# One wide matmul for two products: the feature-major matrix products of a two-block network in float32 pairs

## The chip, the core and the metric

One core of one Trainium2 chip. The metric is device time in microseconds (us) for one execution of the program. TensorE (PE, with its weight loads as PEld) multiplies, VectorE (DVE) and ScalarE (ACT) read its results out of PSUM, GpSimd (POOL) works on SBUF, and SyncE (SP) issues the loads of weights.

## What is computed

256 tokens of 1024 features go through two blocks of two layers each. Cut to what matters:

```python
# first block, per layer
proj = rms_norm(x, norm1_g[l]) @ w_in[l]
x = x + concat([retention(...), stick_breaking(...)]) @ w_out[l]
h = rms_norm(x, norm2_g[l])
x = x + (silu(h @ w_gate[l]) * (h @ w_up[l])) @ w_down[l]
# second block, per layer
proj = rms_norm_2(x, g_mix[l]) @ w_in[l]        # latents, q/k/v of two attentions, gate logits
merged = gates[0] * (y_a @ w_pa[l]) + gates[1] * (y_b @ w_pb[l]) + gates[2] * (y_c @ w_pc[l])
x = x + merged @ w_o[l]
x = x + (silu(h @ w1[l]) * (h @ w3[l])) @ w2[l]  # h = rms_norm_2(x, g_ffn[l])
```

D_FF is 2816 in both blocks, so a feed-forward layer has 22 tiles of 128 hidden features and 8 of output features.

## The kernel before

All operands of the large products are float32 numbers split into two float32r parts, hi and lo (class `Pair`). A product is three matmuls, `mm3` (L253): hi x hi, hi x lo and lo x hi, in lines L255, L256 and L257. The weights come from memory in chunks of 128 x 1024 (`fetch`, L222, on SP's queue, four raw buffers); `split` makes hi on ACT (L237) and lo on DVE (L238), 512 columns at a time, four chunks ahead of their use.

There are two forms of product. In the token-major form (`tm`, L266) the activations are the stationary operand and 512 columns of weights move past them. In the feature-major form (`fm1`, L302, and `fm2`, L281) a weight tile of 128 x 128 is stationary and the 256 tokens of the activations move past it, once for hi and once for lo:

```python
mm(out, l.hi, r.hi, start=start, stop=False, skip_group_check=True)
mm(out, l.hi, r.lo, start=False, stop=False, skip_group_check=True)
mm(out, l.lo, r.hi, start=False, stop=stop, skip_group_check=True)
```

So each of the three lines loads its weight tile anew, the high one twice. `fm2` fills one PSUM bank with two output tiles of 256 columns. PSUM has four banks under the tag mm, two under sc and one each under pt and ov (`bank`, L262).

Feature-major products are: gate and up in `ffn` (L500 to L502, 8 k-tiles), down (L520, 22 k-tiles; the last layer's last two tiles one by one, L524 to L527), sq and sk of the first block's mixer (L578), and in the second block's mixer the gates (L856), q and k of the third attention (L920, L922), the branches (L865, 2 or 4 k-tiles), and w_o (L935). Two latent products go to sc banks (L732). The first block's w_out (L686 to L696) and the second block's latent up-projections (L892 to L913) call `mm3` themselves.

What reads a bank: in `ffn` DVE multiplies G by the row R of 1 / rms (L509), ACT takes silu, DVE multiplies by U (L512), and ACT and DVE split the result into hT's hi and lo (L514, L515). `add` (L447) multiplies by R if given (L454), adds to x (L456), and makes the next norm's xT (L384 on ACT, L385 on DVE) and squares; its instructions and branch c's last ones have a higher priority in the order of instructions. In `branch` (L863) DVE multiplies a bank by the gate (L868, L871); branch a's result is added to mg by POOL (L873), branch c's by DVE (L876), which then makes the pair mT.

The order of each engine's instructions is made by the framework's scheduler from the program's order, the priorities and the buffers that are free; each engine then runs its own instructions in that order.

Of the kernel before, what the change touches and what calls it, by code (L numbers as in the profile page):

```python
# [29 lines left out]
# Position p of the residual holds token TOK[p]: the tokens of one residue mod 4 lie together.  # L30
# [101 lines left out]
def tiles(a):  # L132
    """[256, ...] -> [128, 2, ...]"""
# [43 lines left out]
# ---------------------------------------------------------------- the program  # L177


class Pair:  # L180
    """A float32 tensor as the exact sum of two float32r tensors."""
# [7 lines left out]
    def rearrange(self, *a, **k):  # L189
        return Pair(self.hi.rearrange(*a, **k), self.lo.rearrange(*a, **k))  # L190


class Net:
# [16 lines left out]
    # ---- weights  # L210
# [31 lines left out]
    def chunk(self, inner, ahead=4):  # L242
        """The next chunk of the weights as [128, k-tiles, inner]."""
# [7 lines left out]
    # ---- matrix products  # L251
# [10 lines left out]
    def bank(self, tag="mm"):  # L262
        n = {"mm": 4, "sc": 2, "pt": 1, "ov": 1}[tag]
# [17 lines left out]
    def fm2(self, xT, tag="mm", nk=NKT):  # L281
        """Feature-major product with the next chunks: a bank [128, 2, 256] for two 128-column tiles."""
        out = self.half(tag)
        g = min(CW // 128, nk)
        if CW // (128 * g) >= 2:
            c = self.columns(g)
            for j in range(2):
                for k in range(nk):
                    self.mm3(out[:, j, :], c[:, j, k, :], xT[:, k, :], j + k == 0, k == nk - 1)
        else:  # L290
            for j in range(2):
# [10 lines left out]
    def fm1(self, out, xT, start, nk=NKT):  # L302
        g = CW // 128
        for k0 in range(0, nk, g):
            c = self.chunk(128)
            for k in range(min(g, nk - k0)):
                self.mm3(out, c[:, k, :], xT[:, k0 + k, :], start and k0 + k == 0, k0 + k == nk - 1)

    def evac_pair(self, ps, out, scale=None):
        """A PSUM tensor as an exact pair."""  # L310
# [11 lines left out]
    # ---- small things  # L322

    def gains(self, name, l=0, n=NKT):
        """The columns [128, n] of a gain of layer l."""
# [3 lines left out]
    def rsqrt(self, out, ssq, n):  # L329
        """out = (ssq / n + eps) ** -0.5"""  # L330
# [13 lines left out]
    def transposes(self, src, tag):  # L344
        """src [128 t, 4 * 128] -> a bank [128, 4, 128 t]."""
# [5 lines left out]
    # ---- the residual, its norms, and what is added to it  # L351
# [3 lines left out]
    def norm_start(self, g, natural=False, inner=None, last=False):  # L355
        """A norm of the residual x, k-tile by k-tile: n["T"] becomes x * g, transposed as x is, as a pair.
        What is made of it is still to be scaled by 1 / rms of the token."""
        n = {"g": g, "natural": natural, "inner": inner, "last": last}
        if last:
            n["y"] = self.act.tile([128, NKT, S], F32, tag="xTh", name="y")  # L360
        else:
            n["T"] = self.pair_tile(self.act, [128, NKT, S], "xT")
# [3 lines left out]
    def norm_part(self, n, m):  # L366
        """k-tiles m and m + 1 of x are ready."""
# [38 lines left out]
    def norm_sums(self, n):  # L406
        """The sums over the features, a column for each tile of tokens."""
# [9 lines left out]
    def norm_cols(self, n):  # L417
        """1 / rms as columns [128, 2]; if there is an inner norm, x is to become rms_norm(x, inner) first."""
# [15 lines left out]
    def norm_end(self, n):  # L434
        """1 / rms as columns and as a row on all partitions."""
# [11 lines left out]
    def add(self, b, m, n, R=None):  # L447
        """x += the bank b (scaled by R if given) for k-tiles m and m + 1; the next norm n goes on with them."""
# [606 lines left out]
```

## Time and profile before

| | |
|---|---|
| runs of the program | 1616.18, 1614.48, 1615.78 us; median 1615.78 |
| span of the profiled execution | 1613.9 us |
| PE busy | 1595.7 us, 12188 matmuls |
| PEld busy | 1530.2 us |
| DVE busy | 1049.8 us, 1852 instructions |
| ACT busy | 813.1 us, 1558 instructions |
| read from memory | 266.78 MB, 166 GB/s over the span |

A busy time is the union of an engine's instructions. Matmuls are pipelined: the record of one goes on while the next has begun, so the pace is the distance between starts. In the rows a DVE or ACT instruction is named by what it writes and reads (t<-mm,R), and an idle time by what ended it.

### The profile page before, as it was taken

The page shows a single profiled execution, that of the slowest core. Times are in us where ns is not written, and L with a number is a line of the kernel's source. Part 1 is how long each engine was busy: PE and PEld are TensorE (multiplying, and loading weights), DVE is VectorE, ACT ScalarE, POOL GpSimd, SP SyncE. Part 2 cuts the span into 40 slices and gives each one's busy share as a digit, 9 for nine tenths or more (in the row PEclk, how much of TensorE's full clock was granted, in tenths as well). Part 3 has the DMA queues.
Part 4 walks back from the last instruction along what each step waited for, and adds up shares of the span by engine and source line. Part 5 has one row for each costly group of instructions (what it writes and reads, how often), then busy time and mean ns, then how long its engine had stood idle before and what let it go on. Part 6 is the DMA issues. An engine that isn't in the chain of part 4 may idle for free.

```text
span 1613.9 us, 30319 instructions
## 1 busy us (share of the span) xinstructions
PE 1595.7 (99%) x12188; PEld 1530.2 (95%) x12188; DVE 1049.8 (65%) x1852; ACT 813.1 (50%) x1558; POOL 103.4 (6%) x117
## 2 busy tenths in 40 slices
PE   8999999999999999999999999999999999999997
PEld 7889999997999999899999999999899999999997
DVE  7767565667765656776567766656676567765653
ACT  6545444455554545455444554445455444554442
POOL 2001000100110003100001000001000001100001
PEclk9999999999999999999999999999999999999998
DMA  7445555654455556532534555556532544555551
GB/s 265 171 153 179 183 183 168 197 173 133 163 175 183 181 177 209 181 127 90 183 126 156 183 180 184 180 171 209 177 122 92 183 134 151 181 183 183 177 180 63
DMA packets 78653, 269.81 MB, mean 167 GB/s; under 512 B 8624, under 2 KB 12848, under 8 KB 78384
## 3 DMA queue, kind: packets, MB, share of 16 engines
q1 hardware_dynamic: 78224, 267.34, 50.7%
q8 instruction: 96, 1.57, 0.4%
q10 hardware_dynamic: 288, 0.52, 0.1%
q14 instruction: 45, 0.37, 0.1%
HBM read 266.78 MB, written 1.05 MB: 166 GB/s over the span
## 4 chain that ended last, share of the span: by engine, by line
PE 71%; DVE 0%; POOL 0%; ACT 0%; issue 0%; DVEq 0%; ACTq 0%; POOLq 0%
PE mm L255 21%; PE mm L257 20%; PE mm L256 20%; PE ov L260 3%; PE sc L260 3%; PE pt L348 2%; PE pt L260 1%; PE sc L255 0%; PE sc L256 0%; PE sc L257 0%; PE pt L801 0%; POOL acc L404 0%; DVE y L1018 0%; ACT p L784 0%; POOL rr L335 0%
## 5 line engine op out<-in xcount | busy, mean ns | idle before, releaser
L237 ACT CAST hi<-raw 128x512 fp32r<-128x512 f32 x1004 | 567.7, 611 | 633.7 <-issue 415.8
L238 DVE TENSOR_TENSOR lo<-raw,hi 128x512 fp32r<-128x512 f32 x1004 | 667.6, 701 | 311.6 <-ACT hi L237 308.2
L255 PE MATMUL mm<-xTh,hi 128*128 128x256 f32 x2048 | 582.5, 285 | 0.0
L256 PE MATMUL mm<-xTl,hi 128*128 128x256 f32 x2048 | 581.0, 284 | 0.9 <-DVE xTl L385 0.9
L257 PE MATMUL mm<-xTh,lo 128*128 128x256 f32 x2048 | 581.5, 284 | 0.0
L256 PEld LDWEIGHTS mm<-xTl,hi 128*128 128x128 f32 x2048 | 392.9, 192 | 1.6 <-DVE xTl L385 1.3
L255 PEld LDWEIGHTS mm<-xTh,hi 128*128 128x128 f32 x2048 | 392.5, 192 | 0.5
L257 PEld LDWEIGHTS mm<-xTh,lo 128*128 128x128 f32 x2048 | 392.5, 192 | 0.3
L255 PE MATMUL mm<-hTh,hi 128*128 128x256 f32 x704 | 199.2, 283 | 0.0
L256 PE MATMUL mm<-hTl,hi 128*128 128x256 f32 x704 | 199.2, 283 | 0.0
L257 PE MATMUL mm<-hTh,lo 128*128 128x256 f32 x704 | 199.2, 283 | 0.0
L256 PE MATMUL mm<-lo,xTh 128*128 128x512 f32 (+1 forms) x352 | 136.2, 387 | 1.8 <-DVE lo L238 1.8
L255 PE MATMUL mm<-hi,xTh 128*128 128x512 f32 (+1 forms) x352 | 136.2, 387 | 1.4 <-ACT hi L237 1.4
L257 PE MATMUL mm<-hi,xTl 128*128 128x512 f32 (+1 forms) x352 | 136.4, 388 | 0.0
L255 PEld LDWEIGHTS mm<-hTh,hi 128*128 128x128 f32 x704 | 135.2, 192 | 0.0
L256 PEld LDWEIGHTS mm<-hTl,hi 128*128 128x128 f32 x704 | 135.2, 192 | 0.0
L257 PEld LDWEIGHTS mm<-hTh,lo 128*128 128x128 f32 x704 | 135.2, 192 | 0.0
L256 PEld LDWEIGHTS mm<-lo,xTh 128*128 128x128 f32 x352 | 66.8, 190 | 14.9 <-DVE lo L238 3.3
L255 PEld LDWEIGHTS mm<-hi,xTh 128*128 128x128 f32 x352 | 66.6, 189 | 13.1 <-ACT hi L237 1.9
L257 PEld LDWEIGHTS mm<-hi,xTl 128*128 128x128 f32 x352 | 66.7, 190 | 11.4
L404 POOL TENSOR_TENSOR acc<-acc,sq 128x256 f32<-128x256 f32 x58 | 52.9, 914 | 180.1 <-ACT sq L395 177.9
L512 DVE TENSOR_TENSOR h<-mm,t 128x512 f32<-128x512 f32 x44 | 30.4, 692 | 45.4 <-PE mm L257 42.3
(216 smaller groups left out, 1883.8 us busy)
## 6 DMA issues: line engine op xcount, KB each, us to landing
raw<-w SPq DMA_DIRECT2D x470, 512.0 KB, 3.4
raw<-w SPq DMA_DIRECT2D x32, 384.0 KB, 3.2
bias<-bias SPq DMA_DIRECT2D x16, 256.0 KB, 3.2
c<-c SPq DMA_DIRECT2D x1, 1088.0 KB, 6.4
x<-x SPq DMA_DIRECT2D x4, 256.0 KB, 5.9
c<-c SPq DMA_DIRECT2D x1, 768.0 KB, 7.3
out<-y SPq DMA_DIRECT2D x2, 256.0 KB, 2.3
out<-y ACTq DMA_DIRECT2D x2, 256.0 KB, 2.9
```

The source lines that it names most:

```text
L237: nc.scalar.copy(out=hi[:, c], in_=raw[:, c])
L238: nc.vector.tensor_tensor(out=lo[:, c], in0=raw[:, c], in1=hi[:, c].bitcast(F32), op=ALU.subtract)
L255: mm(out, l.hi, r.hi, start=start, stop=False, skip_group_check=True)
L256: mm(out, l.hi, r.lo, start=False, stop=False, skip_group_check=True)
L257: mm(out, l.lo, r.hi, start=False, stop=stop, skip_group_check=True)
L260: self.nc.tensor.matmul(out, l, r, start=start, stop=stop, skip_group_check=True)
L348: self.nc.tensor.transpose(b[:, k, :], src[:, 128 * k:128 * (k + 1)], self.k["ident"])
L404: nc.gpsimd.tensor_tensor(out=acc, in0=acc, in1=t, op=ALU.add)
L512: nc.vector.tensor_tensor(out=h, in0=U, in1=t, op=ALU.mult)
```

## The change

The hi and lo parts of an activation tensor come to lie side by side in one tile (`Twin`), [128, k, 2, 256]. A feature-major product is then two matmuls (`mmw`): the high weight tile with 512 columns, hi and lo of the activations, into the two halves of a bank, and the low weight tile with the 256 columns of hi into the first half. An output tile takes a bank of its own, a pair of them two banks (`quad`). On the way out ACT copies the second halves to SBUF (`second`) and DVE adds the first halves to them (`whole`); what was done with the bank before is done with the sum. The four mm banks become two buffers of two banks. The weights of gate and up are fetched two chunks of one, then two of the other. The products into sc banks, w_out's and the latents' stay as they are.

```diff
 def lay_ffn(wg, wu, wd):
     out = []
-    for a, b in zip(lay_fm(wg), lay_fm(wu)):
-        out += [a, b]
+    g, u = lay_fm(wg), lay_fm(wu)
+    for j in range(0, len(g), 2):
+        out += g[j:j + 2] + u[j:j + 2]
...
+class Twin(Pair):
+    def __init__(self, t):
+        super().__init__(t[:, :, 0, :], t[:, :, 1, :])
+        self.both = t
...
+    def banks(self):
+        return self.ps.tile([128, 2, 512], F32, tag="mm", bufs=2, name="mm")
...
     def tm(self, xT, nk, n=512, then=None):
-        out = [self.bank() for _ in range(2)]
+        b = self.banks()
+        out = [b[:, i, :] for i in range(2)]
...
+    def mmw(self, out, w, x, k, start, stop):
+        mm = self.nc.tensor.matmul
+        flat = lambda t: t.rearrange("p a t -> p (a t)")
+        mm(flat(out), w.hi, flat(x.both[:, k, :, :]), start=start, stop=False, skip_group_check=True)
+        mm(out[:, 0, :], w.lo, x.hi[:, k, :], start=False, stop=stop, skip_group_check=True)
+
+    def wide1(self, out, xT, nk=NKT):
+        g = CW // 128
+        for k0 in range(0, nk, g):
+            c = self.chunk(128)
+            for k in range(min(g, nk - k0)):
+                self.mmw(out, c[:, k, :], xT, k0 + k, k0 + k == 0, k0 + k == nk - 1)
+
+    def quad(self):
+        return self.banks().rearrange("p e (a t) -> p e a t", a=2)
+
+    def wide2(self, xT, nk=NKT):
+        out = self.quad()
         g = min(CW // 128, nk)
         if CW // (128 * g) >= 2:
             c = self.columns(g)
             for j in range(2):
                 for k in range(nk):
-                    self.mm3(out[:, j, :], c[:, j, k, :], xT[:, k, :], j + k == 0, k == nk - 1)
+                    self.mmw(out[:, j], c[:, j, k, :], xT, k, k == 0, k == nk - 1)
         else:
             for j in range(2):
-                self.fm1(out[:, j, :], xT, j == 0, nk)
+                self.wide1(out[:, j], xT, nk)
         return out
...
+    def second(self, b):
+        t = self.act.tile([128, 2, S], F32, tag="part", bufs=2, name="part")
+        t = t[:, :b.shape[1], :]
+        self.nc.scalar.copy(out=t, in_=b[:, :, 1, :])
+        return t
+
+    def whole(self, out, b):
+        self.nc.vector.tensor_tensor(out=out, in0=b[:, :, 0, :], in1=self.second(b), op=ALU.add)
+        return out
...
             if R is not None:
                 t = self.act.tile([128, 2, S], F32, tag="sq", bufs=2, name="t")
-                nc.vector.tensor_tensor(out=t, in0=b, in1=R.unsqueeze(1).to_broadcast([128, 2, S]), op=ALU.mult)
-                b = t
-            nc.vector.tensor_tensor(out=x, in0=b, in1=x, op=ALU.add)
+                self.whole(t, b)
+                nc.vector.tensor_tensor(out=t, in0=t, in1=R.unsqueeze(1).to_broadcast([128, 2, S]), op=ALU.mult)
+                nc.vector.tensor_tensor(out=x, in0=t, in1=x, op=ALU.add)
+            elif len(b.shape) == 4:
+                t = self.second(b)
+                nc.vector.tensor_tensor(out=x, in0=b[:, :, 0, :], in1=x, op=ALU.add)
+                nc.vector.tensor_tensor(out=x, in0=t, in1=x, op=ALU.add)
+            else:
+                nc.vector.tensor_tensor(out=x, in0=b, in1=x, op=ALU.add)
             self.norm_part(n, m)
...
-                G, U = self.half(), self.half()
-                for e in range(2):
-                    self.fm1(G[:, e, :], xT, e == 0)
-                    self.fm1(U[:, e, :], xT, e == 0)
-                    if j + e == 0:
-                        self.norm_cols(n)
+                G = self.wide2(xT)
+                U = self.quad()
+                self.wide1(U[:, 0], xT)
+                if j == 0:
+                    self.norm_cols(n)
+                self.wide1(U[:, 1], xT)
...
-                nc.vector.tensor_tensor(out=t, in0=G, in1=Rb, op=ALU.mult)
+                self.whole(t, G)
+                nc.vector.tensor_tensor(out=t, in0=t, in1=Rb, op=ALU.mult)
                 nc.scalar.activation(out=t, in_=t, func=AF.Silu)
                 h = pool.tile([128, 2, S], F32, tag="h2", bufs=2, name="h2")
-                nc.vector.tensor_tensor(out=h, in0=U, in1=t, op=ALU.mult)
+                self.whole(h, U)
+                nc.vector.tensor_tensor(out=h, in0=h, in1=t, op=ALU.mult)
...
             def branch(name, nk, th, to=None):
                 for m in range(0, NKT, 2):
-                    b = self.fm2(yT[name], nk=nk)
+                    b = self.wide2(yT[name], nk=nk)
                     c = mg[:, m:m + 2, :]
                     if name == "b":
-                        nc.vector.scalar_tensor_tensor(out=c, in0=th[m // 2], scalar=1.0, in1=b, op0=ALU.add, op1=ALU.mult)
+                        self.whole(c, b)
+                        nc.vector.scalar_tensor_tensor(out=c, in0=th[m // 2], scalar=1.0, in1=c, op0=ALU.add, op1=ALU.mult)
                         continue
                     t = pool.tile([128, 2, S], F32, tag="bias", bufs=3, name="mt")
-                    nc.vector.scalar_tensor_tensor(out=t, in0=th[m // 2], scalar=1.0, in1=b, op0=ALU.add, op1=ALU.mult)
+                    self.whole(t, b)
+                    nc.vector.scalar_tensor_tensor(out=t, in0=th[m // 2], scalar=1.0, in1=t, op0=ALU.add, op1=ALU.mult)
...
-                    b = self.bank().rearrange("p (a t) -> p a t", a=2)
+                    b = self.banks()[:, 0, :].rearrange("p (a t) -> p a t", a=2)
...
```

`add_last`, sq and sk, the gates, and q and k of the third attention are changed like `ffn`'s G: `whole` first, then the operation of before on the sum. The pairs xT, hT, yT and mT become twins; mT takes the place that qa and ka had, which now lie in one tile.

## Rows read from the trace of the kernel before

**Rows 1.** The page, parts 1 and 4: busy times, and the chain that ended last

```profile
span 1613.9 us, 30319 instructions
...
PE 1595.7 (99%) x12188; PEld 1530.2 (95%) x12188; DVE 1049.8 (65%) x1852; ACT 813.1 (50%) x1558; POOL 103.4 (6%) x117
...
PE 71%; DVE 0%; POOL 0%; ACT 0%; issue 0%; DVEq 0%; ACTq 0%; POOLq 0%
```

**Rows 2.** Waits of the weight loads: us in total, times, longest; first and last of 19

```profile
PEld ov L260 <- DVE pT L790: 4.4, 14, 0.3
...
PEld sc L260 <- ACT ka L891: 0.3, 2, 0.2
```

**Rows 3.** Timeline of a down product: start us, us, engine, line, operation

```profile
262.17 0.28 PE L255 MATMUL mm<-hTh,hi 128*128 128x256 f32 x1
262.17 0.19 PEld L256 LDWEIGHTS mm<-hTl,hi 128*128 128x128 f32 x1
...
262.53 0.28 PE L255 MATMUL mm<-hTh,hi 128*128 128x256 f32 x1
```

**Rows 4.** Timeline of token-major products, and of the step to feature-major ones

```profile
400.18 0.39 PE L255 MATMUL mm<-hi,xTh 128*128 128x512 f32 x1
...
400.86 0.39 PE L255 MATMUL mm<-hi,xTh 128*128 128x512 f32 x1
...
807.08 0.39 PE L257 MATMUL mm<-hi,xTl 128*128 128x512 f32 x1
...
807.31 0.28 PE L255 MATMUL mm<-yTh,hi 128*128 128x256 f32 x1
...
807.42 0.28 PE L256 MATMUL mm<-yTl,hi 128*128 128x256 f32 x1
```

**Rows 5.** Busy us of PE, PEld, DVE, ACT, POOL by stretch; PEclk, DMA share, GB/s

```profile
20.00:50.00 30.00, 30.00 (x231) 29.00 (x230) 22.99 (x41) 16.69 (x31) 0.58 (x1) 1.00 0.82 288
134.00:260.00 126.00, 125.58 (x1046) 125.36 (x1046) 75.88 (x123) 60.98 (x110) 2.43 (x3) 1.00 0.55 178
...
864.00:868.00 4.00, 4.00 (x35) 4.00 (x35) 4.00 (x6) 2.06 (x4) 1.68 (x1) 1.00 0.45 146
```

**Rows 6.** Groups by line and form: count, busy us, mean ns

```profile
L255 PE MATMUL mm<-xTh,hi 128*128 128x256 f32 x2048 | 582.5, 285 | 0.0
...
L255 PE MATMUL mm<-hTh,hi 128*128 128x256 f32 x704 | 199.2, 283 | 0.0
```

**Rows 7.** The same groups, for DVE and ACT reading a full bank

```profile
L509 DVE TENSOR_TENSOR t<-mm,R 128x512 f32<-128x512 f32 x44 | 30.4, 691 | 40.5 <-PE mm L257 40.5
...
L646 ACT COPY rk<-pt 128x512 f32<-128x512 f32 x4 | 2.4, 588 | 4.0 <-PE pt L348 4.0
```

**Rows 8.** Timeline of DVE and PE from branch c into w_o, second block, layer 0

```profile
899.49 0.69 DVE L871 SCALAR_TENSOR_TENSOR mt<-th,mm 128x512 f32<-128x512 f32 x1 [1.06 <-PE mm L257]
...
907.86 0.28 PE L255 MATMUL mm<-mT,hi 128*128 128x256 f32 x1
...
908.79 0.68 DVE L871 SCALAR_TENSOR_TENSOR mt<-th,mm 128x512 f32<-128x512 f32 x1
...
909.99 0.69 DVE L876 TENSOR_TENSOR mt<-mg,mt 128x512 f32<-128x512 f32 x1
...
911.37 0.69 DVE L317 SCALAR_TENSOR_TENSOR mT<-mt,mT 128x512 fp32r<-128x512 f32 x1
```

**Rows 9.** Groups: POOL's additions of branch a; timeline: two weight splits on DVE beside them

```profile
L873 POOL TENSOR_TENSOR mg<-mg,mt 128x512 f32<-128x512 f32 x8 | 13.3, 1658 | 349.7 <-DVE mt L871 349.7
...
862.07 2.39 DVE L238 TENSOR_TENSOR lo<-raw,hi 128x512 fp32r<-128x512 f32 x2
```

**Rows 10.** Timeline of PE at the step from w_out to gate and up

```profile
134.81 0.39 PE L256 MATMUL mm<-xTl,hi 128*128 128x256 f32 x1 [0.42 <-DVE xTl L385]
```

**Rows 11.** The chain that ended last, near its end: start us, us, what

```profile
1602.89 0.44 DVE t L464
...
1607.56 0.38 ACT R L1012
```

More of the change, by code (lines that the diff above doesn't have):

```diff
@@ L279, with fm2 @@
     STATS = 1
-    def fm2(self, xT, tag="mm", nk=NKT):
+    def fm2(self, xT, tag, nk=NKT):
         out = self.half(tag)
[L284 to L288, printed above, removed]
-                    self.mm3(out[:, j, :], c[:, j, k, :], xT[:, k, :], j + k == 0, k == nk - 1)
-        else:
-            for j in range(2):
-                self.fm1(out[:, j, :], xT, j == 0, nk)
+        g = CW // 128
+        for j in range(2):
+            for k0 in range(0, nk, g):
+                c = self.chunk(128)
+                for k in range(min(g, nk - k0)):
+                    self.mm3(out[:, j, :], c[:, k, :], xT[:, k0 + k, :], j + k0 + k == 0, k0 + k == nk - 1)
         return out
@@ L306, in fm1 @@
             for k in range(min(g, nk - k0)):
-                self.mm3(out, c[:, k, :], xT[:, k0 + k, :], start and k0 + k == 0, k0 + k == nk - 1)
+                self.mmw(out, c[:, k, :], xT, k0 + k, k0 + k == 0, k0 + k == nk - 1)
[3 more added lines that the diff above has]
+        out = self.quad()
+        g = min(CW // 128, nk)
+        if CW // (128 * g) >= 2:
+            c = self.columns(g)
+            for j in range(2):
+                for k in range(nk):
+                    self.mmw(out[:, j], c[:, j, k, :], xT, k, k == 0, k == nk - 1)
+        else:
+            for j in range(2):
+                self.wide1(out[:, j], xT, nk)
[7 more added lines that the diff above has]
+        self.nc.vector.tensor_tensor(out=out, in0=b[:, :, 0, :], in1=self.second(b), op=ALU.add)
+        return out
     def evac_pair(self, ps, out, scale=None):
@@ L469, in add_last, with half @@
             nc.scalar.mul(out=n["y"][:, j, :], in_=x, mul=n["g"][:, j:j + 1])
[L471 removed]
+    def half(self, tag):
         return self.bank(tag).rearrange("p (a t) -> p a t", a=2)
@@ L519, in ffn @@
                     break
-                self.add(self.fm2(hT, nk=NFT), m, n2, R)
+                self.add(self.wide2(hT, nk=NFT), m, n2, R)
             else:
                 return n2
-            for j in (NKT - 2, NKT - 1):
-                b = self.bank()[:, :S]
-                self.fm1(b, hT, True, NFT)
-                self.add_last(b, j, n2, R)
+            b = self.quad()
+            for j in (0, 1):
+                self.wide1(b[:, j], hT, NFT)
+                self.add_last(b[:, j:j + 1], NKT - 2 + j, n2, R)
             return n2
@@ L577, in mixer1 @@
                 for j in range(2):
-                    b = self.fm2(xT)
-                    nc.vector.scalar_tensor_tensor(out=t[:, 2 * j:2 * j + 2, :], in0=b, scalar=sc, in1=Rb, op0=ALU.mult, op1=ALU.mult)
+                    u = t[:, 2 * j:2 * j + 2, :]
+                    self.whole(u, self.wide2(xT))
+                    nc.vector.scalar_tensor_tensor(out=u, in0=u, scalar=sc, in1=Rb, op0=ALU.mult, op1=ALU.mult)
                 sT.append(t)
@@ L685, in mixer1 @@
                 retention_gate(hp, os[hp])
-            banks = [self.half() for _ in range(NKT // 2)]
+            banks = [t[:, i, :].rearrange("p (a t) -> p a t", a=2) for t in [self.banks() for _ in range(NKT // 4)] for i in range(2)]
             for part in (4, 0):
@@ L855, in gates @@
                     t = pool.tile([128, 2, S], F32, tag="th", bufs=4, name="th")
-                    nc.vector.tensor_tensor(out=t, in0=self.fm2(xT), in1=Rb, op=ALU.mult)
+                    self.whole(t, self.wide2(xT))
+                    nc.vector.tensor_tensor(out=t, in0=t, in1=Rb, op=ALU.mult)
                     nc.scalar.activation(out=t, in_=t, func=AF.Tanh, scale=0.5)
@@ L904, in mixer2 @@
             for j in range(2):
-                b = self.half()
+                b = self.banks()[:, 0, :].rearrange("p (a t) -> p a t", a=2)
                 for e in range(2):
@@ L909, in mixer2 @@
                     nc.scalar.copy(out=kav[p, 2 * j:2 * j + 2, e, :], in_=b[p])
+            b = self.banks()
             for i in range(2):
-                b = self.bank()
-                self.mm3(b, latT[:, 2, 128 * i:128 * (i + 1)], w[:, 1, :], True, True)
-                nc.scalar.copy(out=va[:, i, :], in_=b)
+                self.mm3(b[:, i, :], latT[:, 2, 128 * i:128 * (i + 1)], w[:, 1, :], True, True)
+                nc.scalar.copy(out=va[:, i, :], in_=b[:, i, :])
             wide("a", qa, ka, va, lambda h: h, 96 ** -0.5, None)
@@ L919, in mixer2 @@
             for j in range(2):
-                nc.vector.scalar_tensor_tensor(out=qn[:, 2 * j:2 * j + 2, :], in0=self.fm2(xT), scalar=0.125, in1=Rb, op0=ALU.mult, op1=ALU.mult)
+                u = qn[:, 2 * j:2 * j + 2, :]
+                self.whole(u, self.wide2(xT))
+                nc.vector.scalar_tensor_tensor(out=u, in0=u, scalar=0.125, in1=Rb, op0=ALU.mult, op1=ALU.mult)
             for j in range(2):
-                b = self.fm2(xT)
+                b = self.act.tile([128, 2, S], F32, tag="sq", bufs=2, name="kn")
+                self.whole(b, self.wide2(xT))
                 u = kdv[:, 2 * j:2 * j + 2, :, :]
@@ L930, in mixer2 @@
             branch("a", 4, gates())
-            mT = Pair(*(pool.tile([128, NKT, S], F32R, tag=t, name="mT") for t in ("qa", "ka")))
+            mT = self.twin_tile(pool, NKT, "qk")
             branch("c", 4, gates(), mT)
@@ L934, in mixer2 @@
             for m in range(0, NKT, 2):
-                self.add(self.fm2(mT), m, n2)
+                self.add(self.wide2(mT), m, n2)
             return n2
```

33 lines of the change are left out of this document (18 added, 15 removed).

## The prediction

> **What bounds the kernel now.** I read the page first. TensorE (PE) is busy for 99% of a span of 1613.9 us, and the chain that ended last is 71% PE, with "0%" at every other engine [rows 1]. Matmuls overlap in the records, so a busy share alone does not prove a full engine; the waits of its weight loads do. That list has 19 rows, adds up to some 30 us, and its longest row is 4.4 us in total, its shortest 0.3 us [rows 2]. So PE hardly waits for anybody, and only what shortens its own stream can shorten the run. A microsecond on VectorE (DVE) or ScalarE (ACT) counts only where it makes PE wait.
>
> What paces that stream is read from starts, not from durations. One 256-column product, three matmuls, starts at 262.17 and the next at 262.53 [rows 3]: 120 ns a matmul, though each lasts 280 ns. In a token-major stretch 512-column matmuls start at 400.18 and, three later, at 400.86 [rows 4]: 226.7 ns each. Twice the columns cost 106.7 ns more, which is 256 columns at 2.4 GHz (the granted clock is 1.00 in the gate and up stage [rows 5]). So each weight load with its matmul costs 106.7 ns per 256 columns **plus a fixed 13.3 ns**, at either width, and that fixed part is what the change can save. Where a 512-column matmul is followed by 256-column ones, the starts are 807.08, 807.31, 807.42 [rows 4]: the wide one takes 0.23, the narrow one behind it 0.11 to 0.12. Mixing widths costs nothing extra there.
>
> **The change, part by part.**
>
> *The products.* Per k-tile and 128 output columns three loads and three matmuls of 256 (360 ns) become two loads with matmuls of 512 and 256: 226.7 + 120 = 346.7 ns. The same columns pass, one fixed part is gone: 13.3 ns. The products concerned are those on xT into mm banks (2048) and on hT (704) [rows 6], and by their loops those on yT (2 layers x 8 tiles x (2 + 4 + 4) k-tiles = 160) and mT (2 x 8 x 8 = 128): 3040 in all. The 64 on xT into sc banks, those on mixT and the latents keep three matmuls. 3040 x 13.3 ns = **40.5 us** less, and since PE has no slack to hide it in, all of it is on the path.
>
> The Trainium skill, "TensorE: Matmul & The Clock Gate", section "Back-to-back issue gap", has the isolated gap as N / 2.4 + 2.5 ns, so 109 ns for 256 columns and 216 for 512. The trace disagrees with 120 and 226.7 [rows 3, 4]; by that page of the Trainium skill the saving would be an estimate of 3040 x 2.5 ns = 7.6 us. I keep the trace's number.
>
> *The way out.* Each pair of output tiles now has its two halves in two banks, so it needs one more ACT copy (second) and one more DVE operation (whole, or the second addition in add). Pairs: 88 for gate and up, 15 and two single tiles for down, 8 for sq and sk, and 64 in the second block's mixers: 175 and two singles. An ACT copy of 512 from PSUM lasts 588 ns, a DVE operation of 512 lasts 691 ns [rows 7], but queued DVE operations of that size start 0.60 us apart (three in a row from 908.79 to 909.99, the middle one a weight split [rows 8]). So ACT gains 175 x 0.59 = 103 us and DVE 175 x 0.60 = 105 us: ACT from 813 to 916 us, DVE from 1050 to 1155 us [rows 1], 73% of the new span. Neither becomes the bound as a whole. What matters is each stage.
>
> *Gate and up.* The stretch 134 to 260 has DVE at 75.9 of 126 us [rows 5]. 22 pairs add 13.2 us, so some 89 of 122. A pair's banks are taken again only after the other product has run, 16 x 347 ns = 5.5 us; evacuation needs 0.59 + 0.60. I cost this at nothing; the cover is those 5.5 us, and without it each pair would cost up to 1.2 us. *Down, sq and sk* are the same with 15.3 and 5.5 us per pair: nothing. Token-major products had two of four banks each, now one of two double banks; a product lasts 48 x 226.7 ns = 10.9 us against an evacuation of two operations: nothing. The new order of the weight chunks moves no work: the same chunk arrives every 2.77 us in place of 2.88, 189 GB/s, where the trace has 178 in the gate and up stage and 288 in an early one [rows 5].
>
> *The second block's branches* are the tight place, because there a pair has few k-tiles. Per layer:
> - Branch b (2 k-tiles): PE 4 x 347 = 1.39 us a pair; DVE one weight split, the sum and the product, 3 x 0.60 = 1.80. Over four pairs DVE falls 1.6 us behind. Bounds 0 to 1.6, taken 0.7, as a pair can be one buffer late.
> - Branch a (4 k-tiles): PE 2.77 us a pair. POOL adds into mg at the same time, 1.66 us each [rows 9], and two weight splits then take 2.39 us in place of 1.2; DVE is busy all of 864 to 868 [rows 5, 9]. With sum and product DVE needs 2.39 + 1.20 = 3.6 us a pair: behind by 0.8, over four pairs 3.3. Bounds 0 to 3.3, taken 1.5.
> - Branch c: DVE goes without a gap from 899.49 to 912.06 [rows 8], 12.6 us for 11.5 us of PE. The product after it (w_o) starts at 907.86 and uses k-tiles 0 to 5 of two output tiles first, 12 x 360 ns = 4.3 us, which is just until the last part of mT is written, 911.37 + 0.69 = 912.06. After, the cover is 4.2 us, and DVE has four sums more, 2.4 us, with an ACT copy of 0.6 ahead of the last. Bounds 0 to 3.4 (0 if the weight splits queued in between give way), taken 1.6, the middle, since half of that queue is splits for later chunks.
> - From w_o into the feed-forward: the last addition gets an ACT copy and a DVE addition longer, 0.59 + 0.60 = 1.2 us with a wait. At the same kind of boundary PE already sat 0.42 us waiting for xTl [rows 10]. Bounds 0 to 1.3, taken 0.6.
> - The q projection uses one bank of each double bank, so two in flight, not four. Bounds 0 to 2.7 (four evacuations of 0.69), taken 0.5, near the low end because attention fills PE there.
>
> That is 4.9 us a layer (0 to 12.3), **9.8 us** for two (0 to 24.6); below nothing is excluded, since each of the five only adds instructions or takes buffers away. What waits behind is PE's in-order queue, and next the transposes of attention, whose copies stand in the same DVE queue.
>
> *The tail.* add_last gets a copy of 256 by ACT (0.38, as R's) and a sum by DVE (0.44) on the last chain [rows 11], with issue some **0.9 us**, all exposed.
>
> Sum on the profiled execution: 1613.9 - 40.5 + 9.8 + 0.9 = 1584.1 us. The median of the runs, 1615.78, is 1.9 us above that span, so **1586.0 us**, 1.8% less.
>
> **Rivals.**
> 1. *Evacuation in line (slower).* With two double banks in place of four banks, PE could wait at each pair for copy and sum. Price 1.2 us x 175 = 210 us, less 40.5: 1785 us. It decides from 40.5 / 175 = 0.23 us of exposure per pair. For it: DVE is without a gap in branch c [rows 8]. Against: in gate, up and down, 103 of the pairs, 5.5 us or more pass before a buffer is wanted. Chance 0.04.
> 2. *The saving is not there.* If 120 ns at 256 columns were set by the weight load, and the load behind a narrow matmul held up the next wide one, the change would not do what it says: 1615.8 + 10.7 = 1626.5. For it: a load lasts 0.19 us, more than the 0.12 between starts [rows 3]. Against: the fixed part is the same at 512 columns, where a load has ample time [rows 4]. Chance 0.03. The Trainium skill's 2.5 ns would end close by: 1626.5 less the estimate of 7.6 is 1619.
> 3. *The mixers' queues cost more than the bounds*, 25 to 37 us beside the tail, because instruction order there is chosen anew and attention waits for DVE: 1576 + 25 to 37 = 1601 to 1613. For: DVE is full in the branches [rows 8, 9]. Against: the stretches that are short of DVE today are two of some 12 us a layer. Chance 0.07.
>
> The forecast's own case, 0 to 25 us exposed, has 0.85, and 0.01 remains for a better one.
>
> **The numbers.** The low end takes no exposure but the tail: 1615.8 - 40.5 + 0.9 = 1576, and 1 for run to run: 1575. The high end takes all bounds: 1601. Outside lie rivals 1 to 3, 0.14. A difference of 0.2% (3.2 us) is about the least that a measurement of this kernel can tell from none. Faster by more: 0.85 + 0.07 + 0.01 = 0.93; slower: most of rivals 1 and 2, 0.05; within: 0.02.
>
> **What would show it.** Wide and narrow starts in gate and up alternate at 227 and 120 ns, and a pair of tiles (16 products) takes 5.55 us in place of 5.76; 11 rounds of gate and up take 122 us where they took 126.7. PE's matmul count falls by 3040. ACT is near 916 and DVE near 1155 us. The branches show PE waiting for part, mT or mm banks by 2 to 4 us a layer. I am wrong if the wide start-to-start is over 235 ns, if the feed-forward stages show PE waiting for DVE, or if the mixers lose over 25 us.

## The result and the profile after

The changed kernel takes **1598.26 us** (median of four runs, 1596.3 to 1601.81), against 1615.98 for the kernel before beside it: ratio 0.9896, 95% interval 0.988 to 0.9912. That is 17.7 us less, inside the range, but the predicted gain was 29.8. The profiled execution has a span of 1594.5 us (its own time 1596.3, the shortest of the four), 19.4 less than [rows 1]. One execution of experiment 1 below, which took 8426 us, is left out of its median.

The page of the changed kernel, parts 1, 4 and 5:

```profile
span 1594.5 us, 24578 instructions
...
PE 1564.0 (98%) x9148; PEld 1365.2 (86%) x9148; DVE 1148.7 (72%) x2029; ACT 897.1 (56%) x1735; POOL 110.5 (7%) x117
...
PE 91%; DVE 5%; POOL 1%; ACT 1%; issue 1%; DMA 0%; DVEq 0%; POOLq 0%; ACTq 0%
...
L317 PE MATMUL mm<-xT,hi 128*128 128x512 f32 x2048 | 719.8, 394 | 2.1 <-DVE mt L355 1.2
...
L350 ACT COPY part<-mm 128x512 f32<-128x512 f32 x177 | 102.4, 578 | 9.6 <-PE mm L318 9.6
```

PE's matmuls fall from 12188 to 9148, 3040 as counted. DVE gains 99 us and ACT 84 us. DVE now has 5% of the chain that ended last, where it had none [rows 1].

Timeline of gate and up in the changed kernel (start us, us, engine, line, operation):

```profile
179.66 0.39 PE L317 MATMUL mm<-xT,hi 128*128 128x512 f32 x1
179.89 0.28 PE L318 MATMUL mm<-xT,lo 128*128 128x256 f32 x1
180.01 0.39 PE L317 MATMUL mm<-xT,hi 128*128 128x512 f32 x1
...
181.05 0.39 PE L317 MATMUL mm<-xT,hi 128*128 128x512 f32 x1
```

Four products take 181.05 - 179.66 = 1.39 us, 347 ns each, the wide start to the narrow one 0.23: as predicted, where it was 360 [rows 3]. So the 40.5 us were saved, and 40.5 - 19.4 = **21.1 us came back elsewhere**. Where, is read from the first and last matmul of each stage in the two timelines (us; due: the stage's products times 13.3 ns):

| stage | before | due | after | came back |
|---|---|---|---|---|
| first block, mixer with gate and up, layers 0 and 1 | 260.01, 250.60 | 5.5 less each | 254.54, 245.94 | 0.0, 0.9 |
| down, each of the first three layers | 63.24 | 2.35 less | 60.90 | 0.0 |
| second block, mixer, layer 0 | 293.97 | 5.3 less | 296.20 | 7.5 |
| the same, layer 1 | 289.41 | 5.3 less | 292.78 | 8.7 |
| second block, gate and up (each) | 127.75 | 4.7 less | 123.65, 123.65 | 0.6 each |
| down, last layer | 63.24 | 2.35 less | 62.24 | 1.35 |
| from the last down matmul to the end | 11.41 | none | 12.82 | 1.4 |

Three quarters, 16.2 us, lie in the two mixers of the second block (the row of a mixer begins at the last matmul of the stage before). The waits of the weight loads in the changed kernel (us in total, times, longest) name the places:

```profile
PEld pt L269 <- POOL acc L456: 6.8, 4, 2.2
PEld mm L317 <- DVE qk L366: 6.2, 4, 1.6
PEld mm L317 <- DVE mt L355: 4.5, 6, 1.0
...
PEld mm L317 <- DVE mg L355: 2.8, 6, 0.5
```

The last three did not exist before, where the longest row was 4.4 us [rows 2], and they add up to 13.5 us. All of it is in these two mixers: mg is branch b, mt branch a and the banks that branch c's sums still read, and qk (the tile that mT now lies in) w_o waiting for mT. By stretch, one layer has 1.4 us behind the pairs of branch b, 1.7 behind those of branch a, and 3.1 + 0.6 in w_o. The products of branch c lose nothing (32 products in 11.14 us, from 881.25 to 892.39); what VectorE is late with there is paid in w_o, as PE's timeline of layer 0 shows (in brackets the idle time and what ended it):

```profile
894.40 0.50 PE L317 MATMUL mm<-qk,hi 128*128 128x512 f32 x1 [1.16 <-DVE qk L366]
895.61 0.50 PE L317 MATMUL mm<-qk,hi 128*128 128x512 f32 x1 [0.24 <-DVE mt L355]
900.00 0.50 PE L317 MATMUL mm<-qk,hi 128*128 128x512 f32 x1 [1.32 <-DVE qk L366]
```

The rest of the mixers' loss, 0.6 and 1.5 us, and the first block's 0.9 come ahead of the wide products, at **the step from down into the next mixer**. From the last matmul of down to the first feature-major product of the next mixer the kernel before takes 12.77, 15.76 and 12.07 us, the changed one 13.92, 16.35 and 13.59, which is 3.3 us more. There the last pair's copy and sum stand on the way to x, and behind it come the squares and POOL's sum of them (acc), for which PE waits. It is the first row of the list above; in the kernel before it reads:

```profile
PEld pt L260 <- POOL acc L404: 4.1, 5, 1.7
```

The three steps add up to 40.6 us before and 43.9 after, and to 39.0 and 40.6 in experiments 3 and 4 below, which have no copy and no sum there.

### The profile page after: what moved, and what is told of

Read it like the earlier page. It is cut to its first block, busy times and chain, and to the rows that moved or that the text cites. A ratio compares the mean times of both kernels' runs of the same rounds, so it can differ in the third digit from the quotient of the medians.

```text
span 1594.5 us, 24578 instructions
## 1 busy us (share of the span) xinstructions
PE 1564.0 (98%) x9148; PEld 1365.2 (86%) x9148; DVE 1148.7 (72%) x2029; ACT 897.1 (56%) x1735; POOL 110.5 (7%) x117
## 4 chain that ended last, share of the span: by engine, by line
PE 91%; DVE 5%; POOL 1%; ACT 1%; issue 1%; DMA 0%; DVEq 0%; POOLq 0%; ACTq 0%
PE mm L317 41%; PE mm L318 21%; PE mm L264 6%; PE mm L266 6%; PE mm L265 6%; PE sc L269 4%; PE ov L269 3%; PE pt L400 2%; DVE lo L247 1%; PE pt L269 1%; DVE mt L355 1%; POOL mg L939 1%; DVE mt L937 1%; POOL acc L456 0%; PE sc L264 0%
## 5 line engine op out<-in xcount | busy, mean ns | idle before, releaser
L317 PE MATMUL mm<-xT,hi 128*128 128x512 f32 x2048 | 719.8, 394 | 2.1 <-DVE mt L355 1.2
L318 PE MATMUL mm<-xT,lo 128*128 128x256 f32 x2048 | 577.1, 282 | 0.0
L317 PEld LDWEIGHTS mm<-xT,hi 128*128 128x128 f32 x2048 | 383.3, 187 | 86.8 <-DVE mt L355 1.9
L318 PEld LDWEIGHTS mm<-xT,lo 128*128 128x128 f32 x2048 | 387.1, 189 | 0.8
L317 PE MATMUL mm<-hT,hi 128*128 128x512 f32 x704 | 244.5, 391 | 0.6 <-DVE t L355 0.6
L318 PE MATMUL mm<-hT,lo 128*128 128x256 f32 x704 | 197.1, 280 | 0.0
L264 PE MATMUL mm<-hi,xT 128*128 128x512 f32 (+1 forms) x352 | 137.4, 390 | 1.0 <-ACT hi L246 1.0
L265 PE MATMUL mm<-lo,xT 128*128 128x512 f32 (+1 forms) x352 | 136.8, 389 | 1.5 <-DVE lo L247 1.5
L266 PE MATMUL mm<-hi,xT 128*128 128x512 f32 (+1 forms) x352 | 136.5, 388 | 0.0
L318 PEld LDWEIGHTS mm<-hT,lo 128*128 128x128 f32 x704 | 133.1, 189 | 0.0
L264 PEld LDWEIGHTS mm<-hi,xT 128*128 128x128 f32 x352 | 67.1, 191 | 13.4 <-ACT hi L246 1.5
L266 PEld LDWEIGHTS mm<-hi,xT 128*128 128x128 f32 x352 | 67.0, 190 | 12.0
```

The source lines that it names most:

```text
L317: mm(flat(out), w.hi, flat(x.both[:, k, :, :]), start=start, stop=False, skip_group_check=True)
L318: mm(out[:, 0, :], w.lo, x.hi[:, k, :], start=False, stop=stop, skip_group_check=True)
```

## The experiments

All times are medians beside the kernel before on the same chip. Theory A: the saving belongs to the third load and matmul, and what came back is the work of the way out in stages too short to hide it.

**1. Three loads again, all else changed.** The way out, the banks and the order stay.

```diff
-        mm(flat(out), w.hi, flat(x.both[:, k, :, :]), start=start, stop=False, skip_group_check=True)
+        mm(out[:, 0, :], w.hi, x.hi[:, k, :], start=start, stop=False, skip_group_check=True)
+        mm(out[:, 1, :], w.hi, x.lo[:, k, :], start=False, stop=False, skip_group_check=True)
```

> The changed kernel with its banks, sums and order, but the wide matmul split into two of 256 columns, so that each product loads weights three times again. Theory A (the saving is the fixed part of one load and matmul, 3040 x 13.3 ns = 40 us): 1634 to 1639 us, that is 1598 plus 40 less a few us, because slower products hide some of the mixers' waits; starts 120 ns apart. Rival B (the saving has another source, such as the new order of gate and up or the banks): 1598 to 1610 us.

1633.16 us, ratio 1.0107 (1.009 to 1.0124). Its down stage from the first to the last matmul of hT, by the timeline:

```profile
260.04 0.28 PE L317 MATMUL mm<-hT,hi 128*128 128x256 f32 x1
...
323.28 0.28 PE L319 MATMUL mm<-hT,lo 128*128 128x256 f32 x1
```

63.24 us, the number of before. So the one load and matmul less per product is the whole of the saving, not the banks or the order of the chunks. The run lost 34.9 us (37.8 from profiled span to profiled span), not 40.5: at the slower pace some of the way out hides again. In the list of waits the branches and w_o still have these:

```profile
PEld mm L318 <- DVE qk L367: 2.7, 4, 0.9
PEld mm L317 <- ACT qk L366: 2.6, 4, 0.7
PEld mm L317 <- DVE mt L356: 2.5, 4, 0.7
PEld mm L317 <- DVE mg L356: 1.9, 6, 0.3
```

They are 9.7 us, where the changed kernel has 13.5.

**2. The kernel before with the extra copy and DVE operation,** in its four banks.

```diff
+    def whole(self, out, b):
+        t = self.act.tile([128, 2, S], F32, tag="part", bufs=2, name="part")
+        self.nc.scalar.copy(out=t, in_=b)
+        self.nc.vector.tensor_tensor(out=out, in0=b, in1=t, op=ALU.max)
+        return out
...
-                nc.vector.tensor_tensor(out=t, in0=G, in1=Rb, op=ALU.mult)
+                self.whole(t, G)
+                nc.vector.tensor_tensor(out=t, in0=t, in1=Rb, op=ALU.mult)
```

(and so at every other place where the change has `whole`)

> The kernel before with its three matmuls and four banks, and for each pair of output tiles one more ScalarE copy and one more VectorE operation (the maximum of a bank and its copy, which is the bank). Theory A (the work on the way out costs, whatever the banks): 1625 to 1637 us, with TensorE waiting in the second block's branches. Rival C (the double banks cost, not the work): 1616 to 1619 us.

1628.24 us, ratio 1.0079 (1.0062 to 1.0096), 12.4 us more than 1615.86. The same work costs time with the old banks as well. The time is in theory A's range, but the branches are not where it is lost: in both layers they take 5.75, 11.52 and 11.52 us as in the kernel before, w_o takes 0.4 more, and in place of the four rows of experiment 1 the list has this one:

```profile
PEld mm L256 <- DVE mT L323: 0.6, 2, 0.3
```

What this kernel lost lies at the steps from down into the next mixer (3.3 us in three), from w_o into the feed-forward (4.2 in two) and in the attention between branches a and c (3.2 in two layers). Experiments 1 and 2 do the same work at the same pace of 360 ns a product and differ there in the banks and in where the two halves lie: four single banks have 0.6 us of waits for the way out in branches and w_o, two double ones 9.7. So in the branches it is the work and the loss of buffers together that cost; which part of the new layout it is was not taken apart further.

**3. No copies and no sums,** the second halves of the banks left unread.

```diff
-                self.whole(t, G)
-                nc.vector.tensor_tensor(out=t, in0=t, in1=Rb, op=ALU.mult)
+                nc.vector.tensor_tensor(out=t, in0=G[:, :, 0, :], in1=Rb, op=ALU.mult)
```

(and so at every `whole`, and in `add`)

> The changed kernel without the copies and the sums: what reads a product takes the first half alone, so the product of the low part of the activations is left out of the result; all matmuls stay. Theory A (the 21 us between the 40 us saved on TensorE and the 19 us seen are the work of copies and sums on ScalarE and VectorE): 1575 to 1580 us. Rival C (two double banks in place of four banks, or the joined tiles, make TensorE wait): 1588 to 1598 us.

1602.6 us, ratio 0.9916 (0.9898 to 0.9935): no faster than the changed kernel, which has 177 copies and sums more. Both theories missed. Its waits of the weight loads, and its timeline at the first down stage:

```profile
PEld mm L317 <- DVE t L565: 9.1, 4, 2.3
```

```profile
259.27 0.40 PE L317 MATMUL mm<-hT,hi 128*128 128x512 f32 x1
...
321.34 0.28 PE L318 MATMUL mm<-hT,lo 128*128 128x256 f32 x1
```

Two things had come in with the edit. Without a sum the first pair of gate is multiplied by R straight from its banks, so they are held until R is made: 2.3 us in each of four layers. And after that wait the whole feed-forward ran slower, with no wait in it: 62.07 us for the 176 products of down, 353 ns each, where the changed kernel took 60.90, 347 each. Experiments 4 and 7 follow up on the two.

**4. The same, but the first pair of gate and of up copied and summed,** so that their banks come free before R.

```diff
-                nc.vector.tensor_tensor(out=t, in0=G[:, :, 0, :], in1=Rb, op=ALU.mult)
+                if j == 0:
+                    self.whole(t, G)
+                nc.vector.tensor_tensor(out=t, in0=G[:, :, 0, :] if j else t, in1=Rb, op=ALU.mult)
```

(and so for U)

> As the kernel that took the first halves alone (the low part of the activations left out of the result), but the first pair of gate and of up in each layer is still copied and summed. Theory G (taking the sums away made a new wait: gate's banks were then held until the row R was made, 2.3 us a layer, and after that wait TensorE stayed at 353.3 ns a product where it runs 346.7 in the changed kernel, for the whole feed-forward layer): the wait and the slow pace go, 1575 to 1582 us. Rival C (it was the double banks or the missing sums elsewhere): 1592 to 1603 us.

1581.0 us (1578.52 to 1585.48), ratio 0.979 (0.9774 to 0.9805). Its first down stage:

```profile
260.19 0.39 PE L317 MATMUL mm<-hT,hi 128*128 128x512 f32 x1
...
321.09 0.28 PE L318 MATMUL mm<-hT,lo 128*128 128x256 f32 x1
```

60.90 us again. So the copies and sums, of which this kernel keeps eight, cost about 1598.3 - 1581.0 = 17 us. The profiled execution was the slowest of the four (1585.48) because of its start: its first wide product comes at 28.02 us, that of the changed kernel at 22.49. From there to the end they take 1555.7 and 1572.0 us, 16.4 apart. The two double banks, which this kernel has too, cost little where nothing is to be added up: branches and w_o of layer 0 lose 0.8 us against their pace, where the changed kernel loses 6.9.

**5. The branches alone with three narrow matmuls and one bank,** no copy and no sum there; everything else changed.

```diff
-                    b = self.wide2(yT[name], nk=nk)
+                    b = self.slim2(yT[name], nk)
...
-                    self.whole(t, b)
-                    nc.vector.scalar_tensor_tensor(out=t, in0=th[m // 2], scalar=1.0, in1=t, op0=ALU.add, op1=ALU.mult)
+                    nc.vector.scalar_tensor_tensor(out=t, in0=th[m // 2], scalar=1.0, in1=b, op0=ALU.add, op1=ALU.mult)
```

(`slim2` is the `fm2` of before, in the first bank of a double bank)

> The changed kernel with the three branch products of the second block as before (three matmuls of 256 columns, one bank for a pair, no sum), all else wide. Theory A (branches are where the sums show; their products wait 6.0 us and those of w_o behind them 7.8 us beyond their pace): 1598 + 2.1 - 8 to 14 = 1586 to 1592 us. Rival D (VectorE is late in the whole mixer, and the wait moves to the next product): 1597 to 1601 us.

**1586.25 us**, ratio 0.9816 (0.9801 to 0.983): better than both kernels, 12.0 us below the changed one though it gives 160 x 13.3 ns = 2.1 us of the saving back. Of the three rows above mt and mg are gone, and of qk's 6.2 us this is left in the list of waits:

```profile
PEld mm L317 <- DVE qk L381: 0.4, 2, 0.2
```

w_o itself is unchanged here, so its wait of 3.1 us a layer was made in the branches ahead of it. By the timelines that is branch c, where DVE falls behind.

**6. The sums of branches a and c written over part** instead of into the tile mt, which then is written only by the product with the gate.

```diff
-                    self.whole(t, b)
-                    nc.vector.scalar_tensor_tensor(out=t, in0=th[m // 2], scalar=1.0, in1=t, op0=ALU.add, op1=ALU.mult)
+                    u = self.second(b)
+                    nc.vector.tensor_tensor(out=u, in0=b[:, :, 0, :], in1=u, op=ALU.add)
+                    nc.vector.scalar_tensor_tensor(out=t, in0=th[m // 2], scalar=1.0, in1=u, op0=ALU.add, op1=ALU.mult)
```

The reason is read in branch a of the changed kernel, on DVE and on POOL (timeline; in brackets the idle time and what ended it):

```profile
844.14 0.69 DVE L355 TENSOR_TENSOR mt<-mm,part 128x512 f32<-128x512 f32 x1 [0.31 <-ACT part L350]
...
847.82 0.69 DVE L355 TENSOR_TENSOR mt<-mm,part 128x512 f32<-128x512 f32 x1 [1.19 <-POOL mg L939]
...
851.50 0.69 DVE L355 TENSOR_TENSOR mt<-mm,part 128x512 f32<-128x512 f32 x1 [1.18 <-POOL mg L939]
...
855.17 0.69 DVE L355 TENSOR_TENSOR mt<-mm,part 128x512 f32<-128x512 f32 x1 [0.57 <-POOL mg L939]
```

```profile
846.21 1.59 POOL L939 TENSOR_TENSOR mg<-mg,mt 128x512 f32<-128x512 f32 x1 [171.33 <-DVE mt L937]
849.80 1.67 POOL L939 TENSOR_TENSOR mg<-mg,mt 128x512 f32<-128x512 f32 x1 [2.00 <-DVE mt L937]
```

DVE stands idle 1.19 us for POOL, and the pairs are 3.68 us apart where PE needs 2.77: the sum goes into a tile that POOL's last addition still reads (846.21 + 1.59 = 847.80, and the sum starts at 847.82). DVE has time there; it has no tile to write.

> The changed kernel, but in branches a and c the sum is written over ScalarE's copy (part) and only the product with the gate goes to mt. Theory E (in branch a the sum waits for the mt tile that GpSimd still reads, so that sum, gate and addition follow one another, 3.67 us a pair in the changed kernel's trace against 2.77 us on TensorE): pairs of branch a come 2.8 to 3.2 us apart, 2 to 5 us less in all, 1593 to 1597 us. Rival A (VectorE has too much to do in the branches, whatever tile it writes): 1597 to 1600 us, and 3.4 us or more a pair.

1594.34 us, ratio 0.987 (0.9857 to 0.9884), 3.9 us below the changed kernel. The same four sums in this kernel:

```profile
844.33 0.69 DVE L937 TENSOR_TENSOR part<-mm,part 128x512 f32<-128x512 f32 x1 [0.31 <-ACT part L350]
...
846.74 0.68 DVE L937 TENSOR_TENSOR part<-mm,part 128x512 f32<-128x512 f32 x1
...
849.66 0.68 DVE L937 TENSOR_TENSOR part<-mm,part 128x512 f32<-128x512 f32 x1
...
853.17 0.68 DVE L937 TENSOR_TENSOR part<-mm,part 128x512 f32<-128x512 f32 x1
```

They are 2.4, 2.9 and 3.5 us apart, none waits for POOL, and PE has no wait for the way out left in branch a: its 32 products take 11.09 us. The wait of w_o stays at 6.2 us for both layers: it has another cause, and by the timelines that is DVE's queue in branch c.

**7. What sets the pace of 353 ns?** Two runs. In the changed kernel, with all its copies and sums, the first pair of gate is held for R as in experiment 3:

```diff
-                self.whole(t, G)
-                nc.vector.tensor_tensor(out=t, in0=t, in1=Rb, op=ALU.mult)
+                if j == 0:
+                    p = self.second(G)
+                    nc.vector.tensor_tensor(out=p, in0=p, in1=Rb, op=ALU.mult)
+                    nc.vector.tensor_tensor(out=t, in0=G[:, :, 0, :], in1=Rb, op=ALU.mult)
+                    nc.vector.tensor_tensor(out=t, in0=t, in1=p, op=ALU.add)
+                else:
+                    self.whole(t, G)
+                    nc.vector.tensor_tensor(out=t, in0=t, in1=Rb, op=ALU.mult)
```

> The changed kernel, with the first pair of gate in each feed-forward layer multiplied by R half by half straight from its banks, so that the banks are held until R is there; all copies and sums stay. The changed kernel took 1598.3 us. Theory P, a wait inside the wide stream can put it into the slow pace, where it stays: a wait of some 2.2 us in each of four layers, 8.8 us, and some 496 products a layer at 353.3 in place of 346.7 ns, 13.1 us: 1616 to 1622 with all layers slow, 3.3 us less for each that is not. Theory Q, the slow pace comes from the missing copies and sums: the wait alone, 1605 to 1609, and 346.7 ns throughout.

1619.16 us (ten runs, 1612.4 to 1620.44), ratio 1.0021 (1.001 to 1.0031). The wait, the products just behind it, and the first down stage, in the timeline:

```profile
147.41 0.50 PE L317 MATMUL mm<-xT,hi 128*128 128x512 f32 x1 [1.47 <-DVE h L355]
...
260.57 0.40 PE L317 MATMUL mm<-hT,hi 128*128 128x512 f32 x1
...
322.64 0.28 PE L318 MATMUL mm<-hT,lo 128*128 128x256 f32 x1
```

62.07 us: the slow pace with all copies and sums in place, and so in all four layers. The waits themselves (6.7 us in four) do not make the 21 us; about 13 are the pace.

The other run is experiment 3 with the third pair of gate as three narrow matmuls, to see whether other work ends the slow pace:

```diff
-                G = self.wide2(xT)
+                G = self.slim2(xT, NKT) if j == 2 else self.wide2(xT)
```

> The kernel that adds no second halves (the product with the low part of the activations is left out of the result), with one pair of each feed-forward layer, the third of gate, as three matmuls of 256 columns in one bank. The kernel it is made from took 1602.6 us, and its feed-forward stages ran at 353.3 ns a product after the wait for R. Theory P, the pace is a condition in which the stream stays until something other than wide products passes, and which is then drawn anew: after the narrow pair the 448 products that follow in a layer can go at 346.7 ns, 6.6 ns less each, 11.8 us for four layers, less 0.9 us for 64 more loads: 1590 to 1594 if all four layers return to the fast pace, steps of 3 us for each that does not. Theory Q, the slow pace comes from the missing copies and sums themselves: 353 ns before and after the narrow pair in every layer, 1602 to 1606.

1604.96 us (five runs, 1593.87 to 1606.76), ratio 0.9921 (0.9889 to 0.9952). Down in the first and in the second layer of the profiled execution:

```profile
261.92 0.39 PE L317 MATMUL mm<-hT,hi 128*128 128x512 f32 x1
...
322.82 0.28 PE L318 MATMUL mm<-hT,lo 128*128 128x256 f32 x1
...
573.91 0.40 PE L317 MATMUL mm<-hT,hi 128*128 128x512 f32 x1
...
635.97 0.28 PE L318 MATMUL mm<-hT,lo 128*128 128x256 f32 x1
```

60.90 and 62.06: behind the same sixteen narrow products the first layer went on at the fast pace and the second, like the third and fourth, at the slow one. The time alone is in theory Q's range; what speaks against Q is the pace of the first layer, and with it the run before this one. Of P it holds that the stream can be put into the slow pace and stays in it; that other work draws the pace anew fits the first layer but is not proved by one of four. What decides which pace it will be stays open.

**8. The end of the last layer.** In the changed kernel the last two output tiles share one double bank, and the second stands still until the first has been added up. Given a double bank each:

```diff
-            b = self.quad()
             for j in (0, 1):
-                self.wide1(b[:, j], hT, NFT)
-                self.add_last(b[:, j:j + 1], NKT - 2 + j, n2, R)
+                b = self.quad()
+                self.wide1(b[:, 0], hT, NFT)
+                self.add_last(b[:, 0:1], NKT - 2 + j, n2, R)
```

> The changed kernel with a double bank of its own for each of the last two output tiles. Theory F (the last tile's first matmul waits for the sum of the tile before, because both lie in one buffer; 0.7 us in the changed kernel's trace): that wait is gone, the last layer's down stage takes 60.9 to 61.3 us in place of 62.2. Rival: TensorE waits there for the norm's sums, and the stage stays at 62.2 us.

One run, 1598.79 us; this execution came to its last down stage 4.2 us later than that of the changed kernel (1523.64 against 1519.46; 2.7 of them lie ahead of its first wide product, at 25.20 us), so the stage is what counts. The wait of the changed kernel, and the stage in this one, by the timelines:

```profile
1573.93 0.51 PE L317 MATMUL mm<-hT,hi 128*128 128x512 f32 x1 [0.58 <-DVE t L355]
```

```profile
1523.64 0.39 PE L317 MATMUL mm<-hT,hi 128*128 128x512 f32 x1
...
1584.54 0.28 PE L318 MATMUL mm<-hT,lo 128*128 128x256 f32 x1
```

60.90 us in place of 62.24: the lost 1.35 us of that stage go with this shared buffer. The wait is 0.58 of them; the norm's four small matmuls, which stood in that gap, and the slower pace of the last tile behind it (353 ns, see experiment 7) are in the rest.

**9. Both repairs together,** experiments 5 and 8.

> The branches narrow as before and a double bank for each of the last two tiles. Theory A and F together: the 1586 us of the kernel with narrow branches less 1 to 1.4: 1583 to 1587 us, 1.8 to 2.0% under the kernel before. Rival: no different from narrow branches alone within 1 us, 1586 to 1588.

1585.83 us (five runs, 1583.05 to 1587.03), ratio 0.9812 (0.9799 to 0.9826). The last down stage takes 60.90 us here too, but the difference to experiment 5, 0.4 us, is less than the spread of either. From the first wide product to the end the two profiled executions are 1.0 us apart.

## Why the prediction was right, and where its sizes were wrong

The time came out inside the range, close to its upper end, and partly by luck: the prediction summed 10.7 us of exposure, 21.1 us came back in the profiled execution, and 4.6 of these lie at two places that no term of the sum covers (the step from down into the next mixer, 3.3, and the last two tiles, 1.35). The upper end adds up the bounds of five terms, and one that was not used at all, the 2.7 us a layer of the q projection, left room for them.

**What bounds the kernel** and **the products** held. PE is still the bound (91% of the chain), the pace is 347 ns where 346.7 was predicted, mixed widths cost nothing extra in the undisturbed stream, and putting the third load back puts 63.24 us back into the stage. The Trainium skill's isolated gap of N / 2.4 + 2.5 ns ("TensorE: Matmul & The Clock Gate", "Back-to-back issue gap") gave 7.6 us by an estimate; the stages, where a weight load goes with each matmul, show 40.5 and disagree with that estimate.

**The way out.** ACT ends at 897 (916 predicted) and DVE at 1149 (1155): the counts of instructions were right, but a copy of 578 ns adds only 84 / 177 = 0.47 us, since the records of queued operations of ACT overlap as those of DVE do (in branch c a copy starts at 885.16 us and the operation behind it at 885.63). Gate and up, down, sq and sk, and the token-major products were costed at nothing, and their products lost nothing at their places, as the table shows, but for the last two tiles.

**The step from down into the next mixer** had no term. In `add` the copy and the sum of the last pair lengthen the way to the next norm, as a copy and a second addition do from w_o into the feed-forward, which the prediction did cost. This made 1.2, 0.6 and 1.5 us.

**The branches are the step that failed**, by size. The five terms were summed to 4.9 us a layer; 8.1 and 9.3 us came back, the gate and up stage with them (0.6 and 1.5 of these are the step from down). Term by term, in layer 0 of the second block:
- Branch b: taken 0.7, measured 1.4, inside its bounds of 0 to 1.6.
- Branch a: taken 1.5, measured 1.7, for the wrong reason. The prediction let DVE run short; in fact DVE waits for POOL, as experiment 6 shows. Adding an operation in front of a product moved the moment at which the product's tile is first written forward to the sum, and three buffers were then too few. Attention, whose transposes stand behind in the same queues, adds 0.74 us of waits for pT in that stretch.
- Branch c with w_o: taken 1.6 out of 0 to 3.4, measured 0.6 + 3.1 = 3.7, all of it in w_o and over the upper bound. The value was the middle, on the hope that weight splits in DVE's queue would give way. The trace has DVE without a gap from 885.76 to 899.9, and seven weight splits of that queue stand between the sums.
- From w_o into the feed-forward: taken 0.6, measured 0.6; it is what the rows of gate and up in the table lost, waiting for x and xT.
- The q projection: taken 0.5, and no such wait is in the list.

The mean of a range was taken where the row it was nearest to, DVE without a gap in branch c [rows 8], spoke for the upper end. The upper ends of branches b, a and c add up to 8.3 us a layer; their waits measured 6.8, where 2 to 4 were expected. For the branches the prediction counted VectorE's operations and left the banks to rival 1; experiments 1 and 2 show that both are needed for these waits.

**The tail** was taken at 0.9 and measured 1.4; beside it, 1.35 us were missed altogether, since the two tiles that share a double bank were not looked at (experiment 8).

The sum with the measured terms is 1613.9 - 40.5 + 0.9 + 7.5 + 8.7 + 1.2 + 1.35 + 1.4 = 1594.5 us, the span.

**The rivals.** Evacuation in line (1785 us) did not come: the feed-forward stages keep 347 ns. In the branches, where pairs are short, waits of its kind did come, up to 1.0 us at a pair. "The saving is not there" falls with experiment 1. Rival 3, mixers that lose 25 to 37 us, points the right way and is too big: they lost 16.2.

## What to carry to other kernels

When one engine paces the run, a saving per instruction can be trusted if it is read from the distance of starts, and it was right here to 1%. What is given back is found in the shortest stages: compare, pair by pair, the producer's time with all that each other engine must do, and where the engine that takes over is already without a gap, take the upper bound. If the change also leaves fewer buffers, cost the two together: here the extra work alone left the branches as they were, and the double banks alone cost them and w_o 0.8 us a layer, but both together 6.9 (and still 4.9 of waits at the slower pace of experiment 1). Look at the steps between layers too, where an added operation stands on the way to the next norm. An operation put in front of another also takes its output tile earlier, so count that tile's buffers and who still reads it; and such a change can be made only where stages are long (here all but the branches, 1586.25 us).

## What the runs showed that was not expected

The stream of alternating 512 and 256 columns has **two paces**, 347 and 353 ns a product, at the same granted clock (1.00 in a stretch of gate and up in both kernels), with PE not idle in either. It stays in one of them for a whole feed-forward stage: 60.90 us or 62.07 for 176 products of down. Behind a wait of 1.5 to 2.3 us in gate and up it was the slow one in all eight layers of experiment 3 and of the first run of experiment 7. It also comes without such a wait: in experiment 5 every third wide matmul of a stretch of gates starts at 864.05, 865.11 and 866.17 us, 353 ns a product, and PE has no wait longer than 0.3 us in the fifteen us ahead of it. A layer has 528 such products in its feed-forward, so a layer is 3.5 us longer or shorter by it. The single runs of a kernel with wide products spread over 2.6 to 13 us (most in the second run of experiment 7), where those of the kernel before spread over 3.2 to 4.0. That the pace differs from run to run would explain it. So would the start, while the first weights arrive: in the profiled executions of these kernels the first wide product comes between 22.4 and 28.0 us. Only one execution of each was profiled, so neither is shown.
